# A hybrid encoder block: softmax weights divided inside the transposing matmul, combination rows on a queue of their own, follow-up steps spaced out

## The chip, the cores and the metric

The kernel runs on one core of one Trainium2 chip. A core has five engines that follow their own instruction streams: TensorE (PE, with its weight loads listed as PEld), VectorE (DVE), ScalarE (ACT), GpSimd (POOL) and SyncE (SP, which here only issues DMAs; ACT issues some too). The metric is the device time of one execution in microseconds (us); lower is better.

## The reference, cut to what matters

A pre-norm block on x of 1024 tokens by 2048 columns: one input projection, then windowed grouped-query attention beside a two-way retention scan, both normalised and gated, then one output projection and a final norm. The lines that the change touches are the softmax and its product with V:

```python
s = jnp.where(valid[None, None, None], s + bias[None], -1e30)
m = jnp.maximum(jnp.max(s, axis=-1, keepdims=True), sink_b)
p = jnp.exp(s - m)
p = p / (jnp.sum(p, axis=-1, keepdims=True) + jnp.exp(sink_b - m))
out = jnp.einsum('bhgnqk,bnkhd->bnqhgd', p.astype(v.dtype), vb)
...
h = rmsnorm(x, norm_w[l])
proj = jnp.einsum('bsd,de->bse', h, w_in[l])
...
attn = rmsnorm(attn, attn_out_norm_w[l]) * jax.nn.silu(g_a)
...
mixed = jnp.concatenate([attn.astype(x.dtype), ret], axis=-1)
x = x + jnp.einsum('bse,ed->bsd', mixed, w_out[l])
```

There are 16 query heads in 4 groups of 4, each group with one key and value head; queries come in 8 blocks of 128, and each block sees the 2 or 3 key blocks around it.

## The kernel before, in words

All large products are done as three matmuls on halves of a split number: a value is copied by ACT to a rounded high part (`wh`, `hT`, `PTh`), and DVE or POOL subtract it to get a low part (`wl`, `hT`, `PTl`); line 165 is that copy, line 159 every plain tensor-tensor operation. One group of three 128x512 matmuls is followed by a call of `point()`. The stream of these matmuls has four stages:

- the standard units (lines 1184 to 1186, for `va` 1177 to 1179): K, V and the four Q units, six in all; the tiles of x sit in `hT`
- seven-product units (lines 1007 to 1009): the upper half of the contraction of 16 further units, done as seven products instead of eight. They read *combination rows*: sums and differences of rows of the normalised x, made early, kept in DRAM (`cd`), and loaded back into the 28 rows of `hT` when the x tiles there are no longer needed (`c_load`, `c_split`: one load, one ACT copy, one DVE subtraction for each row). Partial results go to `yd`. Near the stage's end rows of `hT` are refilled from `xd` in the same way, for the next stage
- the half units (lines 1310 to 1312): the lower half of the contraction; each of the 16 units takes its partial result back from `yd` (line 1304) and DVE adds it as it empties the PSUM bank
- the output projection (lines 1363 to 1365, at the end 1385 to 1387)

All else is written as Python generators whose steps are pumped between the groups of matmuls: `point()` takes a step of `jobs` (attention, then its norm, then retention) every `pace` points, of `aux` (sums, rows for the output projection) every `apace` points, and of `post` (what follows a unit) at each point. `drain` runs a queue to a given mark without waiting for points. Stores are put off by some points (`store(..., delay)`). The order of instructions on each engine comes from this order of writing, adjusted by the framework where an instruction's inputs come late; on the chip each engine then takes its instructions strictly in that order, so that a waiting instruction holds up all behind it.

Attention of a group (`attn_job`) runs 32 head-blocks in a software pipeline, one step for each. In step t it issues, where they exist: the product with V of an older pair (lines 582, 583, from `PTh` and `PTl`), the transposes of head-block t-4 (line 597, two or three 128x128 blocks, to PSUM), their split into `PTh` (ACT, line 604) and `PTl` (DVE), then the scores of head-block t (lines 614, 615), the biased maximum (DVE, 623) and the exponentials with their sum (ACT, 627). `normalise(b)` divides a pair: DVE takes the reciprocals of both sums (568) and scales one head's exponentials (570), ACT the other's (571).

When all groups are done, `attn_sum` loads the attention's output in two parts (line 647), waits four steps and adds them (DVE), squares (ACT) and accumulates (POOL); `attn_norm` reduces this with tiny matmuls (line 664), makes the inverse root (POOL and DVE) and spreads it to rows by matmuls (line 185), which go to DRAM as `rbd`. `mixed_row` makes a row for the output projection: for an attention row POOL multiplies gate, `rbd` and row, ACT writes the high part (line 884), DVE the low part (162). At the third half unit `drain` makes sure that the attention's norm is written by then.

Lines of the chain that the prediction uses: 159 (any tensor-tensor operation), 165 (ACT split), 185 and 664 (norm), 597 (transposes), 730, 769, 810 (matmuls and transposes of the retention, plain fp32), 1083 (SiLU of a gate).

## Time and profile before

| | |
|---|---|
| three timed runs | 1544.32, 1547.84, 1550.58 us; median 1547.84 |
| the profiled execution | 1548.5 us; span of the program in it 1546.7 us |
| PE | 1501.8 us busy, 97% of the span |
| DVE, ACT, POOL | 782.9 (51%), 634.0 (41%), 549.3 us (36%) |
| DMA | 292.83 MB, 189 GB/s over the span |
| mean granted clock of TensorE | 0.991 |

The span is from the program's first to its last instruction; what lies around it in the profiled execution is 1.8 us. Matmuls are pipelined: the duration of a record is longer than the distance to the next record's start, and it is this distance that counts in a stream (227 ns for 128x512). A number in brackets in a timeline is idle time of the engine before the instruction, with what ended it.

### The profile page before, as it was taken

The page shows a single profiled execution, that of the slowest core. Times are in us where ns is not written, and L with a number is a line of the kernel's source. Part 1 is how long each engine was busy: PE and PEld are TensorE (multiplying, and loading weights), DVE is VectorE, ACT ScalarE, POOL GpSimd, SP SyncE. Part 2 cuts the span into 40 slices and gives each one's busy share as a digit, 9 for nine tenths or more (in the row PEclk, how much of TensorE's full clock was granted, in tenths as well). Part 3 has the DMA queues.
Part 4 walks back from the last instruction along what each step waited for, and adds up shares of the span by engine and source line. Part 5 has one row for each costly group of instructions (what it writes and reads, how often), then busy time and mean ns, then how long its engine had stood idle before and what let it go on. Part 6 is the DMA issues. An engine that isn't in the chain of part 4 may idle for free.

```text
span 1546.7 us, 21769 instructions
## 1 busy us (share of the span) xinstructions
PE 1501.8 (97%) x7442; PEld 1259.3 (81%) x7442; DVE 782.9 (51%) x1732; ACT 634.0 (41%) x1341; POOL 549.3 (36%) x433
## 2 busy tenths in 40 slices
PE   8999999999999999998999999999999999999997
PEld 6998887778888888887878888888888778878886
DVE  6563335863663663666153635647355434364323
ACT  5311135765774775676212232232323333334210
POOL 3232221347456557445351523525231320112000
PEclk9999999999999999999999999999999999999999
DMA  8879568785445455546656475574635766475403
GB/s 310 296 264 318 190 178 276 240 266 161 143 147 159 152 153 165 158 134 220 216 179 202 136 233 157 161 234 139 224 121 160 250 210 190 157 238 185 125 19 108
DMA packets 185034, 292.83 MB, mean 189 GB/s; under 512 B 28203, under 2 KB 66091, under 8 KB 184284
## 3 DMA queue, kind: packets, MB, share of 16 engines
q1 hardware_dynamic: 152156, 266.28, 53.6%
q10 hardware_dynamic: 32768, 25.17, 5.0%
q8 instruction: 58, 0.95, 0.3%
q14 instruction: 52, 0.43, 0.1%
HBM read 204.84 MB, written 86.54 MB: 188 GB/s over the span
## 4 chain that ended last, share of the span: by engine, by line
PE 78%; DMA 9%; DVE 4%; issue 3%; POOL 3%; ACT 2%; SPq 1%; POOLq 0%; ACTq 0%; DVEq 0%
PE psMa L1310 4%; PE psMb L1310 4%; PE psMa L1312 4%; PE psMa L1311 4%; PE psMb L1311 3%; PE psMb L1312 3%; PE psMa L1007 3%; PE psMa L1008 3%; PE psMa L1009 3%; DMA t<-mpd 2%; PE psMb L1009 2%; PE psMb L1007 2%; PE psMb L1008 2%; PE psST L597 2%; PE psMa L1364 2%
## 5 line engine op out<-in xcount | busy, mean ns | idle before, releaser
L159 POOL TENSOR_TENSOR wl<-r,wh 128x512 fp32r<-128x512 f32 x176 | 233.6, 1330 | 369.4 <-ACT wh L165 344.7
L165 ACT CAST wh<-e 128x512 fp32r<-128x512 f32 x160 | 98.0, 618 | 217.8 <-PE psMb L1365 68.2
L165 ACT CAST wh<-r 128x512 fp32r<-128x512 f32 x176 | 108.2, 617 | 184.1 <-PE psMb L1311 120.5
L159 DVE TENSOR_TENSOR wl<-e,wh 128x512 fp32r<-128x512 f32 x112 | 88.9, 801 | 133.9 <-ACT wh L165 130.8
L159 POOL TENSOR_TENSOR wl<-e,wh 128x512 fp32r<-128x512 f32 x48 | 69.5, 1450 | 206.1 <-ACT wh L165 173.4
L1310 PE MATMUL psMa<-hT,wh 128*128 128x512 f32 x256 | 105.2, 411 | 3.3 <-DVE e L159 3.3
L1007 PE MATMUL psMa<-hT,wh 128*128 128x512 f32 x256 | 102.1, 399 | 4.1 <-DVE e L159 4.1
L1310 PE MATMUL psMb<-hT,wh 128*128 128x512 f32 x256 | 104.5, 408 | 0.0
L1009 PE MATMUL psMa<-hT,wl 128*128 128x512 f32 x256 | 100.8, 394 | 0.0
L1008 PE MATMUL psMa<-hT,wh 128*128 128x512 f32 x256 | 100.7, 393 | 0.0
L1312 PE MATMUL psMa<-hT,wl 128*128 128x512 f32 x256 | 100.5, 393 | 0.0
L1311 PE MATMUL psMa<-hT,wh 128*128 128x512 f32 x256 | 100.4, 392 | 0.0
L1312 PE MATMUL psMb<-hT,wl 128*128 128x512 f32 x256 | 100.0, 391 | 0.0
L1311 PE MATMUL psMb<-hT,wh 128*128 128x512 f32 x256 | 99.9, 390 | 0.0
L627 ACT ACTIVATE P<-P,nmx 128x385 f32<-128x385 f32 (+1 forms) x128 | 75.8, 592 | 35.8 <-DVE nmx L623 33.8
L623 DVE CUSTOM_DVE_ANT_0 P<-psST,bias,nsink 128x384 f32<-128x384 f32 (+1 forms) x128 | 74.3, 581 | 30.4 <-PE psST L615 29.6
L159 POOL TENSOR_TENSOR r<-r,r 128x512 f32<-128x512 f32 x64 | 85.1, 1341 | 3.8
L1007 PE MATMUL psMb<-hT,wh 128*128 128x512 f32 x192 | 76.2, 397 | 0.0
L1009 PE MATMUL psMb<-hT,wl 128*128 128x512 f32 x192 | 75.6, 394 | 0.3 <-POOL wl L159 0.3
L1008 PE MATMUL psMb<-hT,wh 128*128 128x512 f32 x192 | 75.4, 393 | 0.0
L159 DVE TENSOR_TENSOR PTl<-psST,PTh 128x384 fp32r<-128x384 f32 (+1 forms) x128 | 66.5, 519 | 11.3 <-ACT PTh L604 10.8
L159 POOL TENSOR_TENSOR t<-t,t 128x512 f32<-128x512 f32 x32 | 43.4, 1358 | 74.9 <-DMA t<-rbd 42.7
(349 smaller groups left out, 3942.6 us busy)
## 6 DMA issues: line engine op xcount, KB each, us to landing
e<-in_w_out SPq DMA_DIRECT2D x112, 256.0 KB, 3.4
r<-in_w_fast SPq DMA_DIRECT2D x64, 256.0 KB, 3.0
r<-in_w_half SPq DMA_DIRECT2D x64, 256.0 KB, 3.0
e<-yd SPq DMA_DIRECT2D x64, 256.0 KB, 3.8
t<-in_xT SPq DMA_DIRECT2D x31, 512.0 KB, 6.1
e<-in_w_in SPq DMA_DIRECT2D x48, 256.0 KB, 4.5
yd<-e SPq DMA_DIRECT2D x48, 256.0 KB, 2.6
t<-in_x SPq DMA_DIRECT2D x16, 512.0 KB, 6.5
```

Source lines behind the costliest of these rows:

```text
L159: eng.tensor_tensor(o, x, y, op)
L165: A.copy(o_hi, x)
L597: T.transpose(p[:, 128 * i : 128 * i + 128], x[:, 128 * i : 128 * i + 128], ident)
L623: V.tensor_tensor_reduce(x[:, :W], p[:, :W], bias[2 * pr + c][:, k0 : k0 + W], -1.0, nsink[:, head : head + 1], ALU.add, ALU.min, nmx[:, c ...
L627: A.activation(x[:, : W + 1], x[:, : W + 1], AF.Exp, bias=nmx[:, c : c + 1], scale=-1.0, accum_out=sums[:, c : c + 1])
L1007: T.matmul(bank, wh[:, ws], hh, start=(j == 0 and p in (0, 1, 3)), stop=False, skip_group_check=True)
L1008: T.matmul(bank, wh[:, ws], hl, start=False, stop=False, skip_group_check=True)
L1009: T.matmul(bank, wl[:, ws], hh, start=False, stop=(j == 3), skip_group_check=True)
L1310: T.matmul(p, wh[:, ws], hh, start=(w, kk) == (0, 0), stop=False)
L1311: T.matmul(p, wh[:, ws], hl, start=False, stop=False)
L1312: T.matmul(p, wl[:, ws], hh, start=False, stop=last)
L1364: T.matmul(p, mh, wl, start=False, stop=False)
```

## The change

1. `normalise` goes. `divide(j)` makes, two steps after the exponentials of head-block j, a 128x128 diagonal matrix of the reciprocals (DVE: identity times the column of reciprocals, tile `dg`), and the transposes become matmuls of the exponentials with that diagonal, so that each block is transposed and divided at once. The exponentials stay undivided in SBUF.
2. Combination rows: before, in the last standard unit, two rows were split and two loaded at each of the positions from 2 on, and the last two after the unit. Now a generator `rows_in` does one row at a time on a queue `rowq` with a step every 2.4 points, the DVE part a step after the ACT part, in the order 0 to 19, 24 to 27, 20 to 23, and reaches into the seven-product units; those call `drain` for the four rows that they read.
3. Spacing: attention's first group takes a step every 3.0 points, the others every 2.6 (2.62 before); `attn_sum` starts three steps later and leaves five steps between load and addition (four before); `mixed_row` leaves two steps more before the high part of an attention row and one more before every low part; gates are stored with a step more between them and reported six steps later; stores to `yd` are put off by 12 points (7 before); the first half unit takes its PSUM banks in another order; half units load the third and fourth quarter from `yd` two weight tiles in rather than one; the load of queries in attention moves by a step.

The diff, cut to its core:

```diff
-    pt, due, pace, adue, apace = [0], [0], [2.62], [0], [2.0]
+    rowq, rdue = deque(), [0]
+    pt, due, pace, adue, apace = [0], [0], [3.0], [0], [2.0]
...
         pump(post, 1)
+        if rowq and pt[0] >= rdue[0]:
+            rdue[0] = max(rdue[0], pt[0] - 1) + 2.4
+            pump(rowq, 1)
...
+    def rows_in():
+        order = list(range(20)) + list(range(24, 28)) + list(range(20, 24))
+        lo = None
+        for n in range(len(order) + 2):
+            if n < len(order):
+                c_load(0, order[n])
+            if n >= 2:
+                r = order[n - 2]
+                first = 16 * (NS - 1) + r // 2 + 3
+                if step[0] < first:
+                    yield lambda: step[0] >= first
+                lo = c_split(r)
+                yield
+                lo()
+                done.add(("row", r))
+            else:
+                yield
...
-        def normalise(b):
-            n = b % 8
-            W = 128 * (min(n + 2, 8) - max(n - 1, 0))
-            sums = st.pop(b)[1]
-            V.reciprocal(sums, sums)
-            x, y = P[2 * b], P[2 * b + 1]
-            V.tensor_scalar(x[:, :W], x[:, :W], sums[:, 0:1], None, ALU.mult)
-            A.activation(y[:, :W], y[:, :W], AF.Copy, scale=sums[:, 1:2])
+        def divide(j):
+
+            b, c = divmod(j, 2)
+            d = att.tile([128, 128], F32, tag="dg", name=nm("dg"), bufs=3)
+            sums = st[b][1]
+            if c == 0:
+                V.reciprocal(sums, sums)
+            else:
+                st.pop(b)
+            V.tensor_scalar(d, ident, sums[:, c : c + 1], None, ALU.mult)
+            dg[j] = d
...
-                    T.transpose(p[:, 128 * i : 128 * i + 128], x[:, 128 * i : 128 * i + 128], ident)
+                    c0 = slice(128 * i, 128 * i + 128)
+                    T.matmul(p[:, c0], x[:, c0], d, start=(i == 0), stop=True, skip_group_check=True)
...
-                if c == 0 and b:
-                    normalise(b - 1)
...
-            if t == 32:
-                normalise(15)
+            if t >= 2 and t - 2 < 32:
+                divide(t - 2)
             yield
...
     def attn_sum(g):
 
+        for _ in range(3):
+            yield
...
-                for _ in range(4):
+                for _ in range(5):
                     yield
                 tt(V, x, x, y, ALU.add)
...
             tt(G, r, r, g, ALU.mult)
+            yield
+            yield
...
         A.activation(orow(kk, hf, 0), r, AF.Copy, scale=c)
+        yield
         yield
...
     def attention(g):
+        if g == 1:
+            pace[0] = 2.6
...
-            store(yd[q, b], t, t)
+            store(yd[q, b], t, t, None, 12)
...
-                for r in range(2 * pos - 6, 2 * pos - 4):
-                    if r >= 0:
-                        c_split(r)()
-                for r in range(2 * pos - 4, 2 * pos - 2):
-                    c_load(0, r)
+            if last_u and pos == 2:
+                rowq.append((rows_in(), None))
...
+        if u == 0:
+            whole = [whole[0], whole[2], whole[3], whole[1]]
...
-                if w == 1:
+                if w == 1 + b // 2:
```

How the order moves at the three places of which the prediction speaks; line numbers are those of the kernel named.

PE at the attention's norm (L664 and L690 are the tiny sums over `acc`, L185 the spreading to rows; `psMa`, `psMb` with L1310 to L1312, after the change L1342 to L1344, are half units). Before, in the second half unit:

```order
L1312 MATMUL psMa_7996<-hT,wl_7968 128x512
L664 MATMUL psST_8021<-ones,acc 128x2 x8
L1310 MATMUL psMb_7997<-hT,wh_7967 128x512
...
L1312 MATMUL psMa_7995<-hT,wl_8067 128x512
L185 MATMUL psST_8100<-ident,any_8031 128x128 x4
L185 MATMUL psST_8106<-ident,any_8031 128x128 x4
```

After the change:

```order
L1344 MATMUL psMb_8114<-hT,wl_8204 128x512
L690 MATMUL psST_8269<-ones,acc 128x2 x8
L1342 MATMUL psMa_8304<-hT,wh_8239 128x512
L1343 MATMUL psMa_8304<-hT,wh_8239 128x512
L1344 MATMUL psMa_8304<-hT,wl_8240 128x512
L1342 MATMUL psMa_8304<-hT,wh_8239 128x512
L1343 MATMUL psMa_8304<-hT,wh_8239 128x512
L1344 MATMUL psMa_8304<-hT,wl_8240 128x512
L1342 MATMUL psMa_8305<-hT,wh_8239 128x512
L1343 MATMUL psMa_8305<-hT,wh_8239 128x512
L185 MATMUL psST_8287<-ident,any_8279 128x128 x4
L185 MATMUL psST_8293<-ident,any_8279 128x128 x4
```

The sums now stand after the last matmul of the second half unit, just where `drain` asks for them, and 8 large matmuls stand between them and the spreading, where 39 stood before (the three dots hide 37 of those).

DVE where the third half unit's banks are emptied (`e<-psMa`, `e<-psMb`; `qs<-rq,qd` is the first retention's scaled query, which needs a load of `rq`; `hT<-t,ew,hT` the low part of a row for the output projection). Before:

```order
L159 TENSOR_TENSOR e_1706_8086<-e_1706_8086,t_1742_8309 128x512
L162 SCALAR_TENSOR_TENSOR hT<-t_1746_8335,ew,hT 128x512
L159 TENSOR_TENSOR qs_8496<-rq_8450,qd_8458 64x512
L159 TENSOR_TENSOR e_1729_8226<-psMa_8176,e_1729_8226 128x512
L159 TENSOR_TENSOR e_1733_8243<-psMa_8177,e_1733_8243 128x512
```

After the change:

```order
L159 TENSOR_TENSOR e_1833_8222<-e_1833_8222,t_1870_8436 128x512
L162 SCALAR_TENSOR_TENSOR hT<-t_1879_8491,ew,hT 128x512
L159 TENSOR_TENSOR e_1857_8354<-psMa_8304,e_1857_8354 128x512
L159 TENSOR_TENSOR e_1861_8371<-psMa_8305,e_1861_8371 128x512
L159 TENSOR_TENSOR e_1868_8422<-psMb_8306,e_1868_8422 128x512
L159 TENSOR_TENSOR e_1869_8431<-psMb_8307,e_1869_8431 128x512
L159 TENSOR_TENSOR qs_8618<-rq_8576,qd_8584 64x512
```

The scaled query has moved from ahead of the four emptyings to behind them; the low part of the output row still stands ahead.

ACT in the second unit of the output projection (`wh<-e` splits a weight tile, `hT<-t,ew` writes the high part of a row of the second half of the tokens). Before, six such rows stand in this unit; the last three:

```order
L884 ACTIVATE hT<-t_2454_12254,ew 128x512
L165 CAST wh_12202<-e_2438_12160 128x512
L884 ACTIVATE hT<-t_2466_12315,ew 128x512
L165 CAST wh_12222<-e_2441_12181 128x512
L165 CAST wh_12242<-e_2447_12206 128x512
L884 ACTIVATE hT<-t_2480_12390,ew 128x512
```

After the change four stand in it; the last two:

```order
L912 ACTIVATE hT<-t_2579_12372,ew 128x512
L165 CAST wh_12277<-e_2557_12242 128x512
L165 CAST wh_12302<-e_2560_12262 128x512
L912 ACTIVATE hT<-t_2594_12454,ew 128x512
L165 CAST wh_12320<-e_2563_12281 128x512
```

The fifth and sixth row have moved behind the unit's end, eleven weight splits further on.

More of the change, by code (lines that the diff above doesn't have):

```diff
@@ L528, in attn_job @@
         kh, kl, vs = k4(F32R), k4(F32R), k4(F32R)
-        bias, qj, P, PT, st = {}, {}, {}, {}, {}
+        bias, qj, P, PT, st, dg = {}, {}, {}, {}, {}, {}
         def load_bias(h):
@@ L593, in attn_job @@
                 nk = min(n + 2, 8) - max(n - 1, 0)
-                x = P.pop(j)
+                x, d = P.pop(j), dg.pop(j)
                 p = pT()
                 for i in range(nk):
-                    T.transpose(p[:, 128 * i : 128 * i + 128], x[:, 128 * i : 128 * i + 128], ident)
+                    c0 = slice(128 * i, 128 * i + 128)
+                    T.matmul(p[:, c0], x[:, c0], d, start=(i == 0), stop=True, skip_group_check=True)
                 if c == 0:
@@ L629, in attn_job @@
                 )
-                if c == 0 and b:
-                    normalise(b - 1)
                 if t in (4, 16):
                     load_bias(2 if t == 4 else 3)
-                if t % 4 == 0 and t + 4 < 32:
+                if t % 4 == 1 and t + 3 < 32:
                     q_load(t // 4 + 1)
-            if t == 32:
-                normalise(15)
+            if t >= 2 and t - 2 < 32:
+                divide(t - 2)
             yield
     def attn_sum(g):
+        for _ in range(3):
+            yield
         for kk in (2 * g, 2 * g + 1):
@@ L1086, in gate_post @@
             yield
+            yield
+        for _ in range(6):
             yield
@@ L1151, in hybrid_block @@
                 apace[0] = 3.0
-            if last_u and pos >= 2:
-                for r in range(2 * pos - 6, 2 * pos - 4):
-                    if r >= 0:
-                        c_split(r)()
-                for r in range(2 * pos - 4, 2 * pos - 2):
-                    c_load(0, r)
+            if last_u and pos == 2:
+                rowq.append((rows_in(), None))
             if last_u and pos == 7:
@@ L1201, in retention @@
         yield from ret_job(p)
-    for r in range(26, 28):
-        c_split(r)()
     step[0] = 16 * NS
@@ L1229, in between @@
             run_later()
+        if not q:
+            for r in range(4 * p, 4 * p + 4):
+                drain(rowq, ("row", r))
         multiply(q, p, between)
```

## The prediction

> **What bounds the kernel now.** I read the page first, for the busy shares, then busy time and clock by stage, then the waits of TensorE, and last its timeline at single places.
>
> ```profile
> span 1546.7 us, 21769 instructions
> PE 1501.8 (97%) x7442; PEld 1259.3 (81%) x7442; DVE 782.9 (51%) x1732; ACT 634.0 (41%) x1341; POOL 549.3 (36%) x433
> ```
>
> PE is busy for 97% of the span and nothing else for more than about half of it, so an instruction added to PE costs its time, and one taken from DVE or ACT gains only where PE was waiting for it. By stage (us in the stretch, then busy time by engine, then granted clock):
>
> ```profile
> 232.00:349.00 117.00, 106.65 (x540) 89.51 (x540) 78.51 (x203) 78.92 (x187) 36.35 (x28) 0.97 0.82 260
> 349.00:545.00 196.00, 194.22 (x1012) 165.11 (x1011) 105.33 (x287) 126.59 (x298) 118.03 (x91) 1.00 0.49 151
> 545.00:720.00 175.00, 171.81 (x899) 146.58 (x898) 100.95 (x267) 116.33 (x273) 95.39 (x73) 0.99 0.51 156
> 720.00:760.00 40.00, 35.95 (x151) 29.20 (x151) 13.88 (x16) 15.06 (x26) 16.45 (x12) 0.96 0.76 256
> 760.00:815.00 55.00, 52.73 (x247) 43.80 (x246) 22.74 (x33) 9.30 (x16) 28.14 (x23) 0.97 0.56 181
> 815.00:1180.00 365.00, 363.98 (x1892) 304.10 (x1891) 194.54 (x488) 106.48 (x209) 134.83 (x111) 1.00 0.54 175
> 1180.00:1262.00 82.00, 78.32 (x343) 63.08 (x343) 35.02 (x59) 28.57 (x55) 26.05 (x19) 0.98 0.73 238
> 1262.00:1500.00 238.00, 235.81 (x1037) 194.18 (x1036) 103.05 (x160) 80.39 (x155) 27.32 (x22) 1.00 0.50 157
> ```
>
> Stretch less PE's busy time is its idle time: 10.4, 1.8, 3.2, 4.1, 2.3, 1.0, 3.7 and 2.2 us, 28.7 in all. The clock takes more: one minus the clock, times the stretch, is 3.5, 0, 1.8, 1.6, 1.7, 0, 1.6 and 0, 10.2 us. It falls after a wait:
>
> ```profile
> 806.13 0.39 PE L1312 MATMUL psMb<-hT,wl 128*128 128x512 f32 x1
> 808.78 0.76 PE L1310 MATMUL psMa<-hT,wh 128*128 128x512 f32 x1 [2.27 <-DVE e L159]
> 809.35 0.63 PE L1311 MATMUL psMa<-hT,wh 128*128 128x512 f32 x1
> 809.77 0.63 PE L1312 MATMUL psMa<-hT,wl 128*128 128x512 f32 x1
> ```
>
> Behind this wait of 2.27 us two matmuls start 0.42 us apart, where 0.23 is usual (below). So all that the removal of waits can give between 232 and 1500 us is 28.7 + 10.2 = **38.9 us**. This bounds every gain of the change, since nothing in it removes a matmul.
>
> **The diagonal matmul.** The transposes are replaced one for one. Their number and that of two other plain fp32 products:
>
> ```profile
> L597 PE MATMUL psST<-ident,P 128*128 128x128 f32 x352 | 60.1, 274 | 0.0
> L730 PE MATMUL psST<-vt,kT 128*128 128x128 f32 x128 | 16.8, 274 | 0.0
> L810 PE MATMUL psST<-ident,on 128*128 128x128 f32 x64 | 9.6, 272 | 0.0
> L185 PE MATMUL psST<-ident,rcol 128*128 128x128 f32 x16 | 2.1, 281 | 0.4 <-DVE rcol L159 0.4
> ```
>
> The code writes 64 transposes at line 810 (4 pairs of heads, 2 heads, 2 halves, 4 chunks) and 64 matmuls at 730; the first leave 64 records, the second 128. Line 185, with the identity as the moving operand like the new matmul, writes 8 a time and leaves 16. So a plain fp32 matmul is two passes and a transpose one. The new product is fp32 on both sides (`P` and `dg`), so I take two passes. What they take in the stream, four blocks each time, a large matmul on both sides:
>
> ```profile
> 829.95 0.39 PE L1311 MATMUL psMb<-hT,wh 128*128 128x512 f32 x1
> 830.17 0.39 PE L1312 MATMUL psMb<-hT,wl 128*128 128x512 f32 x1
> 830.40 1.05 PE L730 MATMUL psST<-vt,kT 128*128 128x128 f32 x8
> 831.21 0.48 PE L1310 MATMUL psMa<-hT,wh 128*128 128x512 f32 x1
> 831.52 0.40 PE L1311 MATMUL psMa<-hT,wh 128*128 128x512 f32 x1
> ...
> 873.35 0.60 PE L810 MATMUL psST<-ident,on 128*128 128x128 f32 x4
> 873.70 0.48 PE L1310 MATMUL psMb<-hT,wh 128*128 128x512 f32 x1
> 874.01 0.40 PE L1311 MATMUL psMb<-hT,wh 128*128 128x512 f32 x1
> ```
>
> From the first small record to the second large one: 1.12 us for four matmuls, 0.66 for four transposes. A block costs (1.12 - 0.66) / 4 = 0.115 us more, 352 of them **40.5 us**. Less the large matmul's 0.227, a pass takes 0.89 / 8 = 0.112 and a transpose 0.43 / 4 = 0.108. The reading error of 0.01 us on each distance bounds this to 39 to 42 us. No cover hides it where PE is busy; where PE waits it shortens the wait, which the next part counts. This one term is larger than all that there is to gain.
>
> [...]
>
> **What the waits give back.** The division itself:
>
> ```profile
> L570 DVE TENSOR_SCALAR P<-P,sums x64: 353/421/1459, 251.0 to 700.5; 128x384 f32<-128x384 f32 x48, 128x256 f32<-128x256 f32 x16
> L571 ACT ACTIVATE P<-P,sums x64: 493/617/624, 251.0 to 701.6; 128x384 f32<-128x384 f32 x48, 128x256 f32<-128x256 f32 x16
> L421 DVE TENSOR_SCALAR t<-e,lg x8: 278/281/1210, 196.9 to 202.9; 128x128 f32<-128x128 f32 x8
> ```
>
> ACT loses 64 x 0.617 = 39 us, DVE 64 x 0.42 = 27, and DVE gains 128 diagonals at about 0.28 (same shape, line 421) = 36. DVE is hardly relieved, ACT is; the diagonal is ready two steps before PE wants it, so no wait starts there. The 28 loads of the rows move with them on SP, one at a time, so that weight loads stand behind fewer waits for a free tile; the later loads and stores of `yd` pass only loads of the same size. I price both within the next term. In its first stretch attention shares ACT and DVE (79 us busy of 117 each) with the combination rows. Rows one at a time, steps 3.0 points apart, no second scaling on ACT, and 0.23 to 0.35 us more of PE work in each step (two or three blocks) all give `PTh` and `PTl` time. Of 10.4 + 3.5 = 13.9 us I take back 10 (bounds 0 and 13.9; a loss I exclude, since ACT's work falls and the pace is wider). In the other two stretches of attention the pace stays at 2.6 and half of the wait is DVE's: of 1.8 + 3.2 + 1.8 = 6.8 us I take back 2.5 (0 to 6.8).
>
> At 728 us PE waits for a bank behind an addition of the attention's output, which waits for its load:
>
> ```profile
> 728.45 0.39 PE L1009 MATMUL psMb<-hT,wl 128*128 128x512 f32 x1
> 732.89 0.50 PE L1007 MATMUL psMa<-hT,wh 128*128 128x512 f32 x1 [4.05 <-DVE e L159]
> ...
> 730.34 0.69 DVE L159 TENSOR_TENSOR t<-t,t 128x512 f32<-128x512 f32 x1 [2.99 <-DMA t<-mpd]
> ```
>
> A fifth step between load and addition is three points, 9 x 0.227 = 2.0 us, and the changed bank order delays the need. Of 4.1 + 1.6 us I take back 4 (0 to 5.7). At 808 us the emptying of the bank stood behind the scaled query; it now stands ahead, so I take back 2.3 + 1.7 = 4 us.
>
> But what is late next lies just there. Attention now ends later (46 steps of the first group at 0.38 point more), its sums take 27 steps instead of 20 at 3.0 points, 21 points more. The norm therefore slides to the point where it is forced: the tiny sums stand behind the second half unit, with 8 large matmuls, 1.8 us, before the spreading that needs the result. How long the result takes:
>
> ```profile
> 761.89 1.84 PE L664 MATMUL psST<-ones,acc 128*128 128x2 f32 x16
> 764.01 1.67 POOL L159 TENSOR_TENSOR any<-anv,mhalf 128x8 f32<-128x8 f32 x1 [8.27 <-DVE anv L668]
> 768.53 0.17 DVE L159 TENSOR_TENSOR any<-any,ant 128x8 f32<-128x8 f32 x1
> ```
>
> From the end of the sums (763.73) to the last factor (768.70) it is 5.0 us. Before, 39 matmuls (8.9 us) covered it; now PE stands for 5.0 - 1.8 = 3.2 us and by the row at 808 loses another 1.6 to the clock. Queued behind the spreading are the rows' copies on ACT, the store of `rbd`, its loads, POOL's products, and on DVE the low part of an output row ahead of the four emptyings of the third half unit. This chain starts late by 53 matmuls (2888 against 2835 large ones issued), 12 us, and the first emptying has 18 large matmuls, 4.1 us, before its bank is wanted again; a wait at the fourth half unit follows, between 0 and 5 us, and I take 2. New waits: **6.8 us** (0 to 10).
>
> In the output projection (3.7 + 1.6 us) the rows that are forced keep their place between weight splits, so the wait at 1208 us stays; two later rows move out of the second unit. I take back 2 (0 to 5.3). The other stretches I leave as they are: no step of theirs moves by more than a point or two.
>
> Sum: 40.5 - 10 - 2.5 - 4 - 4 - 2 + 6.8 = **+24.8 us**. The profiled execution took 1548.5 us (its span 1546.7), 0.7 above the median of the three runs; 1548.5 + 24.8 - 0.7 = **1573 us** (1.6% more).
>
> **The rivals.** *All waits go and no new one comes.* 1547.8 + 40.5 - 38.9 = 1549 us, no change. For it: every edit of spacing aims at one of the waits listed. Against it: the norm now stands where nothing covers it. *The waits stay or move.* Nothing is taken back but what the longer steps cover (some 5 us), and the new waits come: 1547.8 + 40.5 - 5 + 6.8 = 1590. For it: several waits are for DMA, which the change doesn't lighten. *Not slower, on the other side: one pass.* If the matmul with a diagonal ran as one pass, the first term would be 352 x (0.112 - 0.108) = 1 us and the time 1547.8 + 1 - 15.7 = 1533, faster; with 15.7 us taken back net, it is not slower below 0.045 us more a block. Against it: line 185 has the same shape and the identity, and leaves two records a matmul. [...]
>
> **How the numbers follow.** My forecast has a chance of 0.64, all waits gone 0.10, waits stay 0.21, one pass 0.03, four passes 0.02. The bounds of the single terms run from the second case nearly to 1595. The range of 1553 to 1592 us leaves out most of the case without waits, the two of other pass counts and a part of the third. A difference of 0.5%, 7.7 us, is about what a measurement of this kernel tells from no change: slower than 1555.6 is the forecast but for its lowest edge, the case of staying waits and four passes, 0.86; within 0.5% 0.11; faster 0.03.
>
> **What would show it.** Right: the transposing line with 704 records instead of 352 and PE's busy time up by about 40 us; PE's idle time at 250 to 350 us down to a third; a wait of PE of some 3 us before the spreading of the norm with a dip of the clock behind it; no wait for the scaled query. Wrong: 352 records at that line, or PE's idle time over the whole span near zero, or a wait of tens of microseconds in a place that I called untouched.

## The result, and the profile after

| | before | changed |
|---|---|---|
| timed runs | 1537.96 to 1550.58 us, median 1546.08 (4) | 1588.24 to 1593.18 us, median 1591.52 (4) |
| ratio | | 1.0297, 95% interval 1.0249 to 1.0345 |
| the profiled execution | 1548.5 us, span 1546.7 | 1588.2 us, span 1586.4 |

The change makes the kernel 3% slower: some 45 us by the medians, 39.7 us between the two profiled executions. The forecast was 1573 us; the measured time lies at the upper end of its range, half a microsecond inside it, and within 2 us of the rival in which the waits stay or move (1590).

The head of the changed kernel's page, and the group of the transposing line:

```profile
span 1586.4 us, 22495 instructions
PE 1540.7 (97%) x7794; PEld 1301.1 (82%) x7794; DVE 803.8 (51%) x1796; ACT 606.4 (38%) x1277; POOL 548.9 (35%) x433
L623 PE MATMUL psST<-dg,P 128*128 128x128 f32 x704 | 99.8, 275 | 0.0
```

PE has 352 records more (7794 against 7442), all of them at the transposing line (704 against 352), and is busy for 38.9 us longer. That is nearly the whole difference of the two executions. So PE's waits, which were to pay for a part of it, did not become shorter in sum. By stage, in the same stretches as before:

```profile
232.00:349.00 117.00, 111.63 (x586) 96.03 (x585) 79.94 (x200) 66.84 (x155) 34.67 (x26) 0.97 0.75 246
349.00:545.00 196.00, 195.79 (x1071) 170.48 (x1070) 102.26 (x282) 107.81 (x253) 113.30 (x88) 1.00 0.49 146
545.00:720.00 175.00, 174.93 (x992) 153.64 (x991) 101.99 (x290) 100.38 (x240) 87.05 (x68) 1.00 0.49 146
720.00:760.00 40.00, 37.85 (x205) 32.07 (x204) 28.88 (x60) 27.06 (x59) 17.56 (x14) 1.00 0.70 223
760.00:815.00 55.00, 54.07 (x255) 45.03 (x254) 10.14 (x19) 12.64 (x20) 18.62 (x17) 1.00 0.52 173
815.00:1180.00 365.00, 355.09 (x1815) 295.61 (x1814) 191.04 (x448) 97.65 (x191) 140.46 (x114) 0.99 0.55 175
1180.00:1262.00 82.00, 76.37 (x361) 61.49 (x361) 39.27 (x95) 27.95 (x52) 24.37 (x19) 0.98 0.60 196
1262.00:1500.00 238.00, 234.38 (x1025) 191.56 (x1024) 110.57 (x166) 85.22 (x164) 44.51 (x34) 1.00 0.60 192
```

Idle time of PE (the stretch less its busy time) and what the clock takes (one minus the clock, times the stretch) are now 5.4 + 3.5, 0.2, 0.1, 2.1, 0.9, 9.9 + 3.7, 5.6 + 1.6 and 3.6 us: 36.6 in all, against 38.9 before. (The clock stands with two digits, so that the stretch of 365 us alone can be off by 1.8 us.) The stretch of 815 to 1180 us, where before PE stood for 1.0 us, has taken over what attention gave back. (The later stretches hold a piece of the program that begins some 40 us earlier in it than before; every large wait is told by its place below.) PE's waits that show where:

```profile
PE psMa L1342 <- DVE e L159: 7.0, 2, 6.5
PE psST L836 <- ACT on L825: 2.7, 1, 2.7
PE psMa L1395 <- DVE e L159: 3.6, 2, 2.3
PE psO L607 <- ACT PTh L630: 1.5, 2, 1.1
PE psST L185 <- DVE any L159: 0.9, 1, 0.9
```

The longest single wait inside the program's stream is of 6.5 us. It lies in the half units (line 1342 is line 1310 of before), at the first matmul of the fourth: the same matmul that in the kernel before waited 2.27 us at 808 us. Its timeline on PE, then DVE, ACT, POOL and SP:

```profile
832.46 0.39 PE L1344 MATMUL psMb<-hT,wl 128*128 128x512 f32 x1
839.35 0.76 PE L1342 MATMUL psMa<-hT,wh 128*128 128x512 f32 x1 [6.50 <-DVE e L159]
839.91 0.63 PE L1343 MATMUL psMa<-hT,wh 128*128 128x512 f32 x1
...
837.61 0.98 DVE L162 SCALAR_TENSOR_TENSOR hT<-t,ew,hT 128x512 fp32r<-128x512 f32 x1 [5.19 <-ACT hT L912]
838.52 1.27 DVE L159 TENSOR_TENSOR e<-psMa,e 128x512 f32<-128x512 f32 x2
...
836.86 0.72 ACT L912 ACTIVATE hT<-t,ew 128x512 fp32r<-128x512 f32 x1 [8.97 <-POOL t L159]
...
834.22 2.60 POOL L159 TENSOR_TENSOR t<-t,t 128x512 f32<-128x512 f32 x2 [3.56 <-DMA t<-rbd]
...
816.14 0.33 SPq L900 DMA_DIRECT2D t<-rbd  x1
830.69 0.32 SPq L900 DMA_DIRECT2D t<-rbd  x1
```

Read from the bottom: the norm's factors are loaded for the second row of the output mix at 830.7 us, 14.6 us after the first row's load. POOL can start its two products only when that load has landed, at 834.2; ACT's copy follows at 836.9, and DVE's low part (line 162) at 837.6. Behind it on DVE stand the two emptyings of the banks that PE wants (838.5). PE waits for them, and the clock falls: it is granted at 0.50 from 839.3 to 843.0 us, where it was 1.00 from 826 to 832, and the next matmuls start 0.43 us apart instead of 0.23, for about 4 us. From the last matmul ahead of the wait to the end of the late matmuls the stream takes 8.6 us more than at its usual distances; by the same count the wait of before cost 4.1. In the kernel before the same row's low part was early, and the scaled query behind it was what came last:

```profile
801.57 0.75 DVE L162 SCALAR_TENSOR_TENSOR hT<-t,ew,hT 128x512 fp32r<-128x512 f32 x1 [3.96 <-ACT hT L884]
807.35 0.68 DVE L159 TENSOR_TENSOR qs<-rq,qd 64x512 f32<-64x512 f32 x1 [5.03 <-DMA rq<-rqk]
```

A second new wait is met at the first matmuls of the output projection, 2.3, 1.4 and 0.4 us from 1211 us on, where the kernel before has none (there they start at 1175 us, 0.23 us apart). PE, DVE, ACT and SP:

```profile
1213.34 0.47 PE L1395 MATMUL psMa<-wh,hT 128*128 128x512 f32 x1 [2.25 <-DVE e L159]
...
1211.85 0.75 DVE L162 SCALAR_TENSOR_TENSOR hT<-t,ew,hT 128x512 fp32r<-128x512 f32 x1 [6.10 <-ACT hT L912]
...
1211.09 0.72 ACT L912 ACTIVATE hT<-t,ew 128x512 fp32r<-128x512 f32 x1 [6.38 <-DMA t<-md]
...
1207.99 0.32 SPq L896 DMA_DIRECT2D t<-md  x1
```

Again the low part of an output row, here one of the retention that waits for its load of `md`, stands on DVE ahead of the emptying of the banks; before, it stood behind the emptying of the first two.

### The profile page after: what moved, and what is told of

The parts are those of the page before. It is cut to its first block, busy times and chain, and to the rows that moved or that the text cites. A ratio compares the mean times of both kernels' runs of the same rounds, so it can differ in the third digit from the quotient of the medians.

```text
span 1586.4 us, 22495 instructions
## 1 busy us (share of the span) xinstructions
PE 1540.7 (97%) x7794; PEld 1301.1 (82%) x7794; DVE 803.8 (51%) x1796; ACT 606.4 (38%) x1277; POOL 548.9 (35%) x433
## 4 chain that ended last, share of the span: by engine, by line
PE 79%; DMA 8%; DVE 5%; issue 3%; ACT 2%; POOL 2%; SPq 1%; POOLq 0%; ACTq 0%; DVEq 0%
PE psST L623 4%; PE psMa L1342 3%; PE psMa L1038 3%; PE psMa L1039 3%; PE psMa L1040 3%; PE psMb L1342 3%; PE psMa L1344 3%; PE psMa L1343 3%; PE psMb L1343 3%; PE psMb L1344 3%; PE psMb L1040 2%; PE psMb L1038 2%; PE psMb L1039 2%; PE psST L1397 2%; PE psST L1396 2%
## 5 line engine op out<-in xcount | busy, mean ns | idle before, releaser
L1342 PE MATMUL psMa<-hT,wh 128*128 128x512 f32 x256 | 105.6, 413 | 7.0 <-DVE e L159 7.0
L1342 PE MATMUL psMb<-hT,wh 128*128 128x512 f32 x256 | 104.5, 408 | 0.0
L1344 PE MATMUL psMa<-hT,wl 128*128 128x512 f32 x256 | 101.0, 394 | 0.0
L1344 PE MATMUL psMb<-hT,wl 128*128 128x512 f32 x256 | 100.4, 392 | 0.0
L1343 PE MATMUL psMb<-hT,wh 128*128 128x512 f32 x256 | 100.3, 392 | 0.0
L623 PE MATMUL psST<-dg,P 128*128 128x128 f32 x704 | 99.8, 275 | 0.0
L623 PEld LDWEIGHTS psST<-dg,P 128*128 128x128 f32 x704 | 94.9, 192 | 5.7
L630 ACT CAST PTh<-psST 128x384 fp32r<-128x384 f32 (+1 forms) x128 | 57.9, 452 | 58.3 <-PE psST L623 24.7
L1038 PE MATMUL psMb<-hT,wh 128*128 128x512 f32 x192 | 75.9, 395 | 0.0
```

The lines of the kernel that those rows point to most:

```text
L623: T.matmul(p[:, c0], x[:, c0], d, start=(i == 0), stop=True, skip_group_check=True)
L630: A.copy(hi[:, :nk, c, :], p3)
L1038: T.matmul(bank, wh[:, ws], hh, start=(j == 0 and p in (0, 1, 3)), stop=False, skip_group_check=True)
L1342: T.matmul(p, wh[:, ws], hh, start=(w, kk) == (0, 0), stop=False)
L1343: T.matmul(p, wh[:, ws], hl, start=False, stop=False)
L1344: T.matmul(p, wl[:, ws], hh, start=False, stop=last)
```

## The experiments

The theory after the result (D in the expectations): the diagonal matmul costs its two passes, some 41 us, and the rest of the change nets to about nothing, since attention's waits come back later at rows of the output mix. The rival (S): the diagonal is largely hidden, and the spacing and the moved waits make the kernel slow. All ratios are to the kernel before, run on the same chip beside them. First, each half alone and the pass by itself.

**The change without the diagonal.** `divide` is taken out and `normalise` put back; queue, pace, spacing, bank order and the moved load of queries stay.

```diff
-                    T.matmul(p[:, c0], x[:, c0], d, start=(i == 0), stop=True, skip_group_check=True)
+                    T.transpose(p[:, 128 * i : 128 * i + 128], x[:, 128 * i : 128 * i + 128], ident)
...
+                if c == 0 and b:
+                    normalise(b - 1)
```

> The changed kernel with the division put back as before: the transposes are transposes again, P is scaled on DVE and ACT; the rows' queue, the pace, the spacing and the bank order of the change stay. Theory D (the diagonal matmul is two passes and costs its 41 us of TensorE, and all else nets to about nothing, since the waits that the spacing removes in attention come back at 832, 1033 and 1211 us): 1591.5 - 41 = 1551 us, between 1545 and 1557, 352 records at the transposing line. Rival S (the diagonal is largely hidden, and the spacing and the moved waits make the kernel slow): 1575 to 1590 us.

Measured: 1557.1 us, ratio 1.0066 (1.0036 to 1.0096). The diagonal is worth 34.4 us here. D's number (1551) is missed by 6, S's by 18: what is left of the change, without the diagonal, is not neutral but about 10 us slower than before. The wait of 6.5 us is there as well, at 798 us:

```profile
PE psMa L1340 <- DVE e L159: 6.9, 2, 6.5
PE psO L604 <- ACT PTh L626: 7.1, 5, 2.0
```

So that wait belongs to the spacing and not to the diagonal. Attention's waits for `PTh` are back (second row; 1.5 us in the changed kernel, 5.8 before): the two-pass blocks had covered these. (With the diagonal alone, the next kernel, they are 1.3 us.)

**The diagonal alone.** The kernel before with `divide` and the diagonal matmul, all else as before.

```diff
-                    T.transpose(p[:, 128 * i : 128 * i + 128], x[:, 128 * i : 128 * i + 128], ident)
+                    c0 = slice(128 * i, 128 * i + 128)
+                    T.matmul(p[:, c0], x[:, c0], d, start=(i == 0), stop=True, skip_group_check=True)
```

> The kernel before with the diagonal matmul and its reciprocals alone; loads of rows, pace, spacing and bank order stay as before. Theory D: 1546 + 41 = 1587, less the 3 to 10 us of attention's waits that the longer steps cover: 1577 to 1584 us, 704 records. Rival S: 1546 to 1556 us.

Measured: 1581.9 us, ratio 1.0225 (1.0189 to 1.0261), 34.8 us more than before. In D's band.

**The pass alone.** The kernel before; `normalise` stays, and each transpose is written as a plain matmul with the identity.

```diff
-                    T.transpose(p[:, 128 * i : 128 * i + 128], x[:, 128 * i : 128 * i + 128], ident)
+                    c0 = slice(128 * i, 128 * i + 128)
+                    T.matmul(p[:, c0], x[:, c0], ident, start=(i == 0), stop=True, skip_group_check=True)
```

> The kernel before with every transpose of P written as a plain fp32 matmul with the identity as the moving operand; the scaling on DVE and ACT stays, so only the number of passes changes. Theory D (the price is the second pass on TensorE, whatever the diagonal holds): as diagonal_only within 6 us, 1577 to 1588 us, TensorE's busy time up by 39 us. Rival: if the diagonals' work on DVE and the later point of the division are what costs, this kernel stays at 1546 to 1555 us.

Measured: 1582.2 us, ratio 1.0215 (1.0178 to 1.0252): the same as the diagonal alone. The page's second row and the group of the line:

```profile
PE 1541.7 (97%) x7794; PEld 1303.6 (82%) x7794; DVE 786.6 (50%) x1732; ACT 637.3 (40%) x1341; POOL 551.1 (35%) x433
L598 PE MATMUL psST<-ident,P 128*128 128x128 f32 x704 | 99.8, 275 | 0.0
```

DVE and ACT do what they did before, and the loss is there in full. The price is the second pass on PE; what the diagonal holds, and how it is made, costs nothing that can be measured.

**The change without its spacing.** Sums, mixed rows, stores and bank order as before; the diagonal, the rows' queue, the pace and the moved load of queries stay. The gates are not as before: the kernel before already leaves two steps after each gate's store, and the change only adds the six at the end; this edit takes out one of the two as well, so that the gates are stored closer together than in either kernel and reported four steps earlier than before. (It is so in every experiment below that undoes the gates.)

```diff
-        for _ in range(3):
-            yield
         for kk in (2 * g, 2 * g + 1):
...
-                for _ in range(5):
+                for _ in range(4):
...
-            yield
-            yield
         for _ in range(3):
...
-            store(yd[q, b], t, t, None, 12)
+            store(yd[q, b], t, t)
...
             store_now(gd[128 * c : 128 * c + 128, 512 * hf : 512 * hf + 512], t)
-            yield
-            yield
-        for _ in range(6):
             yield
...
-            whole = [whole[0], whole[2], whole[3], whole[1]]
```

> The changed kernel without its spacing: sums of attention, mixed rows, gate products and stores at the distances of before, and the bank order of before; the diagonal, the rows' queue and the pace stay. Theory D: the waits at 832, 1033 and 1211 us (about 9.5, 3 and 6 us with their dips of the clock) become small again, and the one at 728 us (5.7) and that for the scaled query at 808 us (4) return: 1591.5 - 18 + 10 = about 1583, between 1577 and 1592 us. Rival S: 1550 to 1570 us.

Measured: 1581.1 us, ratio 1.0210 (1.0176 to 1.0244). That is the diagonal alone (1581.9): the spacing costs 10 us, and the rows' queue and the pace nothing in sum. The change without the diagonal gives the same 10 us with the gates left as in the change. As D expected, the wait at the half unit shrinks (2.4 us at 833, with 1.2 more at 764) and that of the addition of attention's output returns (3.0 us at 757). Against D, the waits at the start of the output projection stay (2.5, 1.4 and 0.4 us from 1201 us on), so they don't come from the spacing.

The next question was which part of the spacing makes the new wait: the sums, which put the norm off (N), or the steps inside a row (M).

**Sums spaced as before.**

```diff
-        for _ in range(3):
-            yield
         for kk in (2 * g, 2 * g + 1):
...
-                for _ in range(5):
+                for _ in range(4):
```

> The changed kernel with the sums of attention's output spaced as before (no three steps ahead, four steps between load and addition instead of five); all else of the change stays. Theory N (the wait of 6.5 us at 832 us comes from the norm being late, so that the load of the norm's factors, issued behind the stores of the rotated keys, and with it POOL's product, the row's copy and its low part on DVE are late ahead of the bank's emptyings): that wait falls to under 3 us, 6 to 8 us are gained, of which up to 4 are lost again at the wait of the addition near 750 us: 1584 to 1589. Theory M (it comes from the three more steps inside a row): the wait stays at 6 us or more, 1590 to 1594.

Measured: 1586.1 us, ratio 1.0257 (1.0231 to 1.0283).

**Rows spaced as before.**

```diff
             tt(G, r, r, g, ALU.mult)
-            yield
-            yield
         for _ in range(3):
...
         yield
-        yield
         stt(V, orow(kk, hf, 1), r, c, orow(kk, hf, 0).bitcast(F32), ALU.mult, ALU.subtract)
```

> The changed kernel with the rows of the output mix spaced as before (two steps fewer ahead of the copy, one fewer ahead of the low part); all else of the change stays. Theory N: the wait at 832 us stays at 6 us or more, since the low part cannot start before the norm's factors have landed wherever it stands; the wait at 1033 us (2.7) may go, since the tile that DVE's shuffle waits for there is held by such a row; 1588 to 1593 us. Theory M: the wait at 832 us falls under 3 us, 1580 to 1585.

Measured: 1594.7 us, ratio 1.0305 (1.0276 to 1.0335), 1.7 us above N's band. The wait at the half unit in the timeline of the first and then of the second kernel, with the two loads of the norm's factors in the first:

```profile
832.69 0.77 PE L1340 MATMUL psMa<-hT,wh 128*128 128x512 f32 x1 [2.62 <-DVE e L159]
...
812.37 0.33 SPq L898 DMA_DIRECT2D t<-rbd  x1
823.96 0.32 SPq L898 DMA_DIRECT2D t<-rbd  x1
```

```profile
838.78 0.76 PE L1339 MATMUL psMa<-hT,wh 128*128 128x512 f32 x1 [6.52 <-DVE e L159]
```

With the sums back the second load is issued 6.7 us earlier, PE wants the bank 2.8 us earlier, and the wait falls by about the difference, from 6.5 to 2.6 us: to about what it was before the change (2.3). With the rows' own steps back it stays as it was: the low part cannot start before the factors have landed, wherever it is written. N holds. The times agree in direction (-5.4 and +3.1 us), but their intervals overlap that of the changed kernel, so it is the rows of the timeline that decide. N had thought that the wait at 1033 us might go with the rows' steps; it grew from 2.7 to 5.1 us. And N had the addition's wait return with the sums; in that kernel's trace it doesn't.

**The gates, or the banks?** That wait at 1033 us was still there with the sums back (3.1 us). In that kernel, DVE, then POOL, ACT and PE:

```profile
1018.47 0.01 DVE L1131 LOAD_MASK_SELECT t<-e  x1 [4.08 <-POOL t L159]
1020.27 1.25 DVE L807 TENSOR_SCALAR bnv<-bmv 128x4 f32<-128x4 f32 x1
...
1017.14 2.67 POOL L159 TENSOR_TENSOR t<-t,t 128x512 f32<-128x512 f32 x2 [2.59 <-DMA t<-rbd]
...
1028.48 1.65 ACT L823 ACTIVATE on<-on,bnt,bny 128x128 f32<-128x128 f32 x4 [7.41 <-DVE bnt L162]
...
1029.03 1.49 PE L834 MATMUL psST<-ident,on 128*128 128x128 f32 x4 [3.08 <-ACT on L823]
```

DVE stands for 4.1 us before a shuffle for the rotation, until POOL has worked on a row of the mix, and stands ahead of the retention's small statistics, which ACT's normalising and then PE's transposes want. Three of these small operations are slow there as well: the 1.25 us shown, then 0.93 and 1.21 us behind it, where the kernel before has 0.17 at the same place; POOL works on large tiles beside them (the last section is about this). A row is let in when its gate is reported done. Two kernels, both with the sums as before: in the first the gates and stores go back as well (the gates beyond where they were, as said above), in the second the bank order.

```diff
-            store(yd[q, b], t, t, None, 12)
+            store(yd[q, b], t, t)
...
             store_now(gd[128 * c : 128 * c + 128, 512 * hf : 512 * hf + 512], t)
-            yield
-            yield
-        for _ in range(6):
             yield
         done.add((kind, i))
```

> The changed kernel with the spacing of the sums and of the gate products undone and the stores of the quarters delayed as before; the later rows and the bank order of the change stay. no_late_sums took 1586 and had waits of 3.2 and 1 us at 1026 to 1036 (ScalarE's normalising behind a DVE that waits for a tile of a mixed row). If the gates' six more steps shift the rows onto that place, these waits and their dip of the clock go: 1586 - 6 = 1580, the same as no_spacing (1581). If the row's own steps or the bank order do it, they stay: 1584 to 1588.

```diff
-            whole = [whole[0], whole[2], whole[3], whole[1]]
...
-                if w == 1 + b // 2:
+                if w == 1:
```

> The changed kernel with the spacing of the sums and the bank order undone; gates, stores and rows stay spaced as in the change. If the gates shift the rows, the wait at 1026 us stays (3 us) and the wait for a bank near 764 us returns (1.2): 1585 to 1588. If the bank order makes the wait at 1026 us, it goes: 1580 to 1583.

Measured: 1581.7 us (ratio 1.0240, 1.0197 to 1.0282) and 1587.0 us (1.0270, 1.0235 to 1.0305). In the second the wait for ACT's normalising stays (2.7 us); the first has none for it, and its small operations are back at 0.17 us, but it has 1.9 us for a bank at 1008 and 2.6 us for the addition near 759. It is the gates (or the stores that go with them in this run) that shift the rows onto that place, not the banks. How much of the wait comes of DVE's standing for POOL and how much of the three slow operations (2.9 us) no run separates. By time the gain of some 4 us has an interval that overlaps; with it the time is that of the kernel without any spacing.

**The rest of the change alone.** The kernel before with the rows' queue, the paces and the moved load of queries (the gates with one step less after each store, as above), and the same with the change's bank order.

```diff
+    rowq, rdue = deque(), [0]
+    pt, due, pace, adue, apace = [0], [0], [3.0], [0], [2.0]
...
+            if last_u and pos == 2:
+                rowq.append((rows_in(), None))
...
+        if g == 1:
+            pace[0] = 2.6
...
             store_now(gd[128 * c : 128 * c + 128, 512 * hf : 512 * hf + 512], t)
-            yield
             yield
         done.add((kind, i))
```

> The kernel before with only the rows' own queue and the paces of the change: transposes and the scaling of P as before, no spacing, bank order of before. From no_spacing (1581) less the 35 us that the diagonal cost alone: 1546 us, the same as before within 4 us. If the queue and the pace take back attention's waits (by no_spacing's trace some 8 of 17 us between 250 and 350 us) and lose nothing elsewhere: 1538 to 1541.

```diff
+        if u == 0:
+            whole = [whole[0], whole[2], whole[3], whole[1]]
...
-                if w == 1:
+                if w == 1 + b // 2:
```

> As rows_queue_and_pace, and also with the bank order of the change in the first unit of the output's input product, and the quarters' loads split over two weight steps. In no_spacing, whose bank order is that of before, TensorE waits for a bank at 764 (1.2 us) and 833 us (2.4); if the order removes them, 3 to 5 us faster than rows_queue_and_pace; if the banks only wait at another place, the same within 3 us.

Measured over ten runs each: 1546.6 us, ratio 0.9998 (0.9984 to 1.0012), and 1547.9 us, 1.0009 (0.9992 to 1.0025). Neither changes the time. That isn't because nothing moved. In the first kernel the wait for the addition at 728 us (4.05 us before) is gone, though the sums are spaced as before, and the one at the start of the output projection has come:

```profile
1170.17 0.77 PE L1383 MATMUL psMa<-wh,hT 128*128 128x512 f32 x1 [2.67 <-DVE e L159]
```

It stands, with 2.3 to 3.5 us, in every kernel here that has the queue and the pace, and in none without them (0.4 us at most), so it belongs to this part of the change. The hoped-for 8 us of attention's waits are not there: with steps of the old length, PE's matmuls still start 13.8 us later in sum between 250 and 350 us than their usual distances would have it (16.8 before).

**One pass.** To price the rival of one pass, P and the matrix are held in the reduced format of the large matmuls, first with the diagonal, then with the identity and `normalise`.

```diff
-                x = att.tile([128, 388], F32, tag="P", name=nm("P"), bufs=4)
+                x = att.tile([128, 388], F32R, tag="P", name=nm("P"), bufs=4)
...
-            d = att.tile([128, 128], F32, tag="dg", name=nm("dg"), bufs=3)
+            d = att.tile([128, 128], F32R, tag="dg", name=nm("dg"), bufs=3)
```

> The kernel before with the diagonal matmul alone, as in diagonal_only, but with P and the diagonal held in the reduced fp32 format of the large matmuls. It leaves out the low part of the scores, of the exponentials and of the reciprocals. It prices the rival of one pass. If one record is left a block, with a length in proportion to the large matmul's 0.227 us for 512 columns, a block takes 0.057 us against a transpose's 0.108: 352 x 0.051 = 18 us less than before, 1529, or with the waits of attention that shorter steps uncover 1530 to 1540, 352 records. If a narrow product in this format takes as long as two passes of plain fp32, 1580 us.

```diff
+        idr = att.tile([128, 128], F32R, tag="idr", name=nm("idr"), bufs=1)
+        A.copy(idr, ident)
...
+                    T.matmul(p[:, c0], x[:, c0], idr, start=(i == 0), stop=True, skip_group_check=True)
```

> As one_pass_diagonal, but with P scaled on DVE and ScalarE as before and the identity as the moving operand; it leaves out the low part of the scores and exponentials, as that one does. one_pass_diagonal left one record a block, 0.09 us apart, and still took 1558, since TensorE waited 17 us for the reduction of the scores (nmx) on DVE, where a diagonal took 0.53 us. If the diagonals' place and time on DVE make that wait, it falls here to the 2 us of before, and the time is that of before less the shorter blocks (352 x 0.015 = 5 us): 1540 to 1546. If shorter steps alone uncover it, the wait stays above 10 us: 1553 to 1560.

Measured: 1558.6 us (ratio 1.0098, 1.0066 to 1.0130) with the diagonal and 1557.7 us (1.0051, 1.0035 to 1.0067) with the identity. Three of the four expectations miss; the fourth (a wait above 10 us, 1553 to 1560) is met by the identity in number. The group of the line in the first, and its longest waits:

```profile
L601 PE MATMUL psST<-dg,P 128*128 128x128 f32 x352 | 53.5, 255 | 0.0
PE psST L618 <- DVE nmx L627: 17.3, 13, 4.0
```

There is one record a block, but it is no shorter in the stream than a transpose. From the first of three blocks to the second score matmul behind them it takes 0.51 us, the median of 63 such places; it is 0.50 with transposes (62 places) and 0.85 with two passes (64, the changed kernel). So one pass saves the price of the second and gains nothing beyond, and the fourth expectation's reason, shorter steps, is not what the trace shows. That the kernels are still 9 to 14 us slower than before is waits in attention, and they don't come from the diagonals alone, since they are there with the identity too (10.5 us for `nmx`, in an execution that was the slowest of its seven). A sample of one of these waits from the diagonal's kernel, DVE then PE:

```profile
333.44 0.69 DVE L159 TENSOR_TENSOR t<-t,t 128x512 f32<-128x512 f32 x1 [5.69 <-DMA t<-mpd]
334.31 0.61 DVE L627 CUSTOM_DVE_ANT_0 P<-psST,bias,nsink 128x384 fp32r<-128x384 f32 x1
...
334.98 0.44 PE L618 MATMUL psST<-k,qj 128*128 128x384 f32 x1 [4.02 <-DVE nmx L627]
```

The maximum of the scores stands on DVE behind an addition that waits 5.7 us for its load. Why these loads come later with the reduced format than before, with the same work on PE, was not found.

No version that was run beats the kernel before.

## Why the prediction was right, and where it was not

**What bounds the kernel** held: PE is at 97% before and after, and what was added to it came out at the end: it is busy for 38.9 us more, and the execution takes 39.7 us more.

**The diagonal matmul, +40.5 us**, held in the trace and in the runs. Two records a block; 0.114 us more a block by the distances above ((0.845 - 0.504) / 3) against the forecast 0.115; PE's busy time up by 38.9. By the medians the diagonal alone costs 34.8 (29 to 40), the identity alone 35.1, and the two agree. No run shows the four passes to which the prediction gives a chance of 0.02: the changed kernel leaves two records a block, 704 for 352 blocks, and a block's two take 0.224 us for 128 columns, about what 512 columns of the reduced format take (0.227).

**The waits** are where the sum went wrong. Forecast and measured, from the two tables by stage (idle time and clock together):

| stretch | forecast | measured |
|---|---|---|
| attention, 232 to 349 us | -10 | -5.0 |
| attention, 349 to 720 | -2.5 | -6.5 |
| 720 to 760 (bank behind the addition) | -4 | -3.6 |
| 760 to 815 (scaled query -4, spreading +4.8) | +0.8 | -3.1 |
| 815 to 1180 (fourth half unit) | +2 | +12.6 |
| 1180 to 1500 (output projection) | -2 | +3.4 |
| sum | -15.7 | -2.2 |

- Attention as a whole gave back 11.5 us of the 12.5 forecast, but less than forecast in its first stretch and more in the others. It took both means together: PE's waits for `PTh`, `PTl`, `nmx` and `P` are 14.8 us before and 7.7 in the changed kernel, but 13.0 with the diagonal alone and 12.6 with the queue and the pace alone (one execution each).
- The wait at 728 us went, as forecast, but not for the reason I gave, the fifth step between load and addition: it is gone too in two kernels with the sums spaced as before, the change with only its sums undone and the queue and the pace alone.
- The scaled query no longer holds the bank, as forecast; but the matmul that it held is the first of the fourth half unit, the same that the next term is about. I took back 4 us there and added 2; it now costs 8.6 us where it cost 4.1.
- The wait ahead of the norm's spreading, forecast as 3.2 us and another 1.6 to the clock, was 0.9 us, and the clock stayed (1.00 from 806 to 818 us). I carried the latency of 5.0 us over from an execution where two of its small operations were slow for another reason (below); here it was 2.8 us.
- **The step that failed** is "a wait at the fourth half unit follows, between 0 and 5 us, and I take 2". The mechanism was the right one, a late norm with an output row's low part ahead of the emptyings, and the run with the sums as before confirms it. But its size doesn't follow from its own numbers: 12 us late less 4.1 of cover is 7.9, and I wrote "between 0 and 5" and took 2 without a reason. What delays the bank is the second row of the mix, whose load of the factors is issued 16.8 us after the first row's before and 14.6 after, so that it carries the whole lateness of the norm. Its low part started 5.0 us before the bank was wanted (801.57 against 806.51 us) and now starts 4.8 us after (837.61 against 832.85), 9.7 us later. The wait is 6.5 us, and I put no fall of the clock on it; with that it is 8.6. The term was +2 and measured about +8.6.
- "The other stretches I leave as they are: no step of theirs moves by more than a point or two" was wrong. Each gate is now reported six steps later (they are not stored with a step more between them, as my list of the change says: two steps stand there in both kernels). That puts rows of the mix in front of the retention's statistics, a wait of 2.7 us at 1033 us and its fall of the clock (0.50 from 1038 to 1041 us). I had priced the yields of the gates at nothing without naming what hides them.
- In the output projection the wait of before at 1208 us stayed, as forecast (1.3 and 0.4 us before, 1.2 and 0.4 at 1247 us now), and the three behind weight splits at 1248 to 1259 us (2.0 us together) went on with the rows that moved, to 1326 to 1346 us (1.8). What I had not seen is the new wait at its first matmuls (2.3, 1.4 and 0.4 us with a fall of the clock, 0.50 from 1215.7 to 1218.4 us), which comes with the queue and the pace.
- By place, in the sum of how much later PE's matmuls start than the median distance of the same pair in the same trace: the spacing's two places cost 4.3 and 1.0 us before and 8.8 and 6.7 in the changed kernel (fourth half unit, retention's statistics), 10 us more, which is what the runs price it at. The start of the output projection costs 6.3 instead of 0.4, and the addition at 728 us nothing instead of 5.2.
- Of the signs that I named, the 704 records and PE's busy time held; PE's idle time at 250 to 350 us fell to half (10.4 to 5.4 us) and not to a third, and the wait before the spreading with its dip of the clock did not come in that size.

The sum with the measured terms: 352 x 0.114 = 40.1, less 2.2, is 37.9 against 39.7 between the two executions; the rest is within the rounding of the clock. The medians lie 45 apart, since the profiled execution is the fastest of the changed kernel's four runs, and that of before lies 2.4 us above its median. The runs split the 45 into about 35 for the second pass and 10 for the spacing. That the range held is luck: its upper end is 0.5 us above a median whose runs spread over 5 us, and the forecast itself, 1573, is 18 us off.

Of the rivals, "waits stay or move" is the one that came, with 1590 against 1591.5: the waits moved. The number is in part chance, since the rival took back 5 us and added 6.8, while attention alone gave back 11.5. Its reason, that several waits are for DMA, which the change doesn't lighten, fits the two new ones at 833 and 1211 us, which go back to loads of `rbd` and `md`. "One pass" would not have given 1533 either: with transposes, one record a block, the rest of the change is at 1557.

## What to carry to other kernels

A plain fp32 matmul with the identity or a diagonal in place of a transpose of 128x128 blocks costs 0.114 us a block in this stream; folding a scaling into it pays only where PE has that time to spare, however much it takes off other engines (here 27.6 us off ACT; DVE got 20.9 us more). When steps are put further apart to remove one wait, follow every later step of the same chain to the next place where its engine's queue is shared with something that PE needs, the last row of it and not the first. Try each part of such a bundle by itself: here one part cost 35 us, one 10, and two changed nothing in the time, one of them, by its trace, because it lost at one place what it saved at others. A part that is undone must be undone to what stood before: four kernels here have gates that stand in neither the kernel before nor the change.

## What the runs showed of the hardware that I had not expected

Small operations on DVE were slow while POOL worked on a large tile, 1.25 and 1.30 us against 0.17. The norm's factors in the kernel before, DVE then POOL, and the same operations in the changed kernel:

```profile
765.71 1.25 DVE L159 TENSOR_TENSOR ant<-anv,any 128x8 f32<-128x8 f32 x1 [1.78 <-POOL any L159]
766.99 0.17 DVE L159 TENSOR_TENSOR ant<-ant,any 128x8 f32<-128x8 f32 x1
767.19 1.30 DVE L178 TENSOR_SCALAR ant<-ant 128x8 f32<-128x8 f32 x1
...
765.65 1.29 POOL L159 TENSOR_TENSOR wl<-r,wh 128x512 fp32r<-128x512 f32 x1
767.18 1.29 POOL L159 TENSOR_TENSOR wl<-r,wh 128x512 fp32r<-128x512 f32 x1 [0.24 <-ACT wh L165]
```

```profile
810.13 0.17 DVE L159 TENSOR_TENSOR ant<-ant,any 128x8 f32<-128x8 f32 x1
810.33 0.17 DVE L178 TENSOR_SCALAR ant<-ant 128x8 f32<-128x8 f32 x1
```

The two long ones begin and end with POOL's products of 1.29 us; between them, and where POOL does no product, the same operation takes 0.17. So the median misleads for such operations: the diagonals, which I had priced at 0.28 us, have a median of 0.288 but take up to 1.38, and 0.55 in the mean (the changed kernel's 128). Of these the 54 that no POOL instruction of over 1 us overlaps take 0.27 to 0.29 us, the other 74 take 0.27 to 1.38. No run here changes POOL's work alone, so that POOL is what holds them up is read from the times and not shown.

A matmul of 128 columns in the reduced fp32 format takes as long as an fp32 transpose in the stream (0.51 against 0.50 us for three with a score matmul behind them), not a quarter of the 0.227 us of 512 columns, on which my estimate of 0.057 rested. In the kernel with the diagonal a group of three takes 0.28 us up to the first score matmul behind it (402.17 to 402.45 us), 0.09 a block. What holds the blocks that far apart was not tested.
